# Moving the start of every large operand in on-chip memory: 32 bytes into a 256-byte line, 224 for one set of weights

## The chip, the core and the metric

The kernel runs on one core of a Trainium2 chip. The core has a matrix engine (TensorE, in the profile PE for the products and PEld for the loading of the operand that stays in the array), VectorE (DVE), ScalarE (ACT), GpSimd (POOL) and SyncE (SP), which here only issues transfers. The on-chip memory has 128 partitions; a tile's row is a run of bytes that begins at the same address in every partition. The metric is the device time of one execution in microseconds. The time before is 1136.45 us, the median of 3 runs (1136.25 to 1136.63).

## The reference

One layer of a decoder trunk on 256 tokens of 2048 features, all in float32:

```python
h = rms_norm(x, norm1_g)
proj = h @ w_in                      # 2048 x 6152: q, k, v of two groups of 8 heads, 8 forget logits
y_a = fox_attention(q_a, k_a, v_a, log_sigmoid(f_a + forget_b))
y_b = dilated_attention(q_b, k_b, v_b, rel_bias)
mixed = concat(rms_norm(y_a, outnorm_a_g), rms_norm(y_b, outnorm_b_g))
x = x + mixed @ w_out                # 2048 x 2048
h = rms_norm(x, norm2_g)
x = x + square(relu(h @ w_mlp_in)) @ w_mlp_out   # 2048 x 8192, 8192 x 2048
out = rms_norm(x, final_norm_g)
```

## The kernel before

**Products.** Every float32 matrix is split into a high and a low part of the type float32r, and each product is made of three: high by high, low by high, high by low. Activations are kept turned, with features on the partitions: `aT_hi` and `aT_lo` hold 16 blocks of 128 features by 256 tokens, `big_hi` and `big_lo` the same for the attention's output and later for the hidden layer. Weights come in steps of 256 rows by 512 columns: a transfer brings two steps into a `raw` tile, ACT copies one step into `whi` (L168), DVE subtracts to get `wlo` (L169). Both are tiles of four rotating buffers, and a step holds two blocks of 128 rows (index `j`).

In the input projection, the output projection and the down projection (L299 to L301) the weights are the *moving* operand, which streams through the array 512 columns at a time, and 128 tokens of an activation block are the *stationary* one, loaded before each product. In the up projection (L313) it is the other way: 128 columns of the weights are stationary, and the 256 tokens of a block of `aT` move. So the input projection moves `whi`/`wlo` past `aT`, output and down move `whi`/`wlo` past `big`, and up moves `aT` past `whi`/`wlo`.

**Order.** The order on every engine is written out by hand: a loop over 376 steps issues a step's products, and a table of side jobs by product (attention, norms, draining of accumulators) puts the rest between them. The splitting runs 3 steps ahead of the products, the transfers two to four steps ahead of that. The stages follow one another as input projection (with the attention of a group of heads beside the next chunks), output projection, then four rounds of up and down. The last chunk of the last down is done in three pieces; the high and low weights of its first four steps lie in the memory of `aT`, which is free by then, and its last two pieces are 256 columns wide.

**Addresses.** Tiles come from pools, and a pool's tiles lie one behind the other in the order in which they are first asked for, each rounded up to 32 bytes. So the small tiles between the large ones (norm statistics of 8 bytes, a bias of 32) decide where a large one begins. What begins where within 256 bytes, by the built program:

| operand | before | after |
|---|---|---|
| `aT_hi`, `aT_lo` | 224 | 32 |
| `big_hi`, `big_lo` | 160 | 32 |
| `whi`, `wlo` in input, output and down projection | 160 | 32 |
| `whi`, `wlo` in the up projection | 160 | 224 |
| queries, values (stationary in the attention's L493, L538) | 224 | 0 |
| keys, probabilities (moving there) | 32 | 0 |
| `xs`, identity | 128 | 0 |
| `raw` buffers | 160, 32, 160, 32 | 0, 128, 0, 128 |

All blocks within a tile lie 512, 1024 or 2048 bytes apart, so a product's operand begins at the same place of a 256-byte line as its tile. For moving / stationary this makes 160/224 in the input projection, 160/160 in output and down, 224/160 in up and 32/224 in the attention's products.

The lines that the prediction speaks of, beside L168 and L169, are these:

```python
# L299-L301, input, output, down: stationary xh/xl, moving hi/lo
nc.tensor.matmul(acc, xh, hi[:, j, cols], start=go, stop=False)
nc.tensor.matmul(acc, xl, hi[:, j, cols], start=False, stop=False)
nc.tensor.matmul(acc, xh, lo[:, j, cols], start=False, stop=end)
# L313, up: stationary 128 columns of the weights, moving 256 tokens
nc.tensor.matmul(acc, w[:, j, b * P:(b + 1) * P], a[:, kt, :], ...)
```

L538 multiplies values by probabilities (256 columns, then 128), L333 the 16 forget columns, L544 and L546 square and sum the attention's output through the tile `sqt`.

Of the kernel before, what the change touches and what calls it, by code (L numbers as in the profile page):

```python
# [11 lines left out]
F32 = mybir.dt.float32  # L12
F32R = mybir.dt.float32r
# [6 lines left out]
P = 128  # L20
# [16 lines left out]
QSCALE = HD ** -0.5  # L37

LEAD = 3
WARM, WARM2 = 8, 1  # L40


def _constants():
    i = np.arange(P)
    upto = (i[:, None] <= i[None, :]).astype(np.float32)
    after = (i[:, None] > i[None, :]).astype(np.float32)
    tri = np.where(i[None, :] <= i[:, None], 0.0, NEG).astype(np.float32)
    head = (i[:, None] % 32 == np.arange(NH)[None, :]).astype(np.float32)
    pack = np.concatenate([after, -upto, tri, np.zeros((P, P), np.float32), tri, head], axis=1)

    dist = np.arange(RW) - 127
    d = np.maximum(dist, 0)
    exact = N_BUCKETS // 2
    df = np.maximum(d.astype(np.float32), np.float32(1.0))
    large = exact + (
        np.log(df / np.float32(exact)) / np.float32(math.log(REL_MAX / exact)) * np.float32(N_BUCKETS - exact)
    ).astype(np.int32)
    bucket = np.where(d < exact, d, np.minimum(large, N_BUCKETS - 1))
    count = np.zeros(RW, np.int64)
    for window, dil in PATTERNS:  # L60
        count += (dist >= 0) & (dist % dil == 0) & (dist <= window)
# [7 lines left out]
def kernel(  # L69
# [20 lines left out]
    o2d = out.rearrange("b (t p) d -> p (b t) d", p=P)  # L90
    w_in, w_out, w_up, w_down = w_in[0], w_out[0], w_mlp_in[0], w_mlp_out[0]

    one = ctx.enter_context(tc.tile_pool(name="one", bufs=1))
    two = ctx.enter_context(tc.tile_pool(name="two", bufs=2))
    wraw = ctx.enter_context(tc.tile_pool(name="wraw", bufs=4))
    wsplit = ctx.enter_context(tc.tile_pool(name="wsplit", bufs=LEAD + 1))
    psum = ctx.enter_context(tc.tile_pool(name="psum", bufs=2, space=PSUM))
    dram = ctx.enter_context(tc.tile_pool(name="dram", bufs=1, space=DRAM))
    ctx.enter_context(tc.manual_schedule())
# [44 lines left out]
    def split(i, j0=0, n=2):  # L144
        if i >= len(steps):
            return
        if j0:
            return split_rows(i, j0, n)
        ci, s = steps[i]
        t = raws[ci, s // 2][:, 2 * (s % 2):2 * (s % 2) + 2, :]  # L150
        if ci == len(chunks) - 1 and s < 4:
            hi, lo = (a[:, 4 * s:4 * s + 4, :].rearrange("p (k j) s -> p k (j s)", k=2) for a in (aT_hi, aT_lo))
        else:
            hi, lo = (wsplit.tile([P, 2, CW], F32R, name=n) for n in ("whi", "wlo"))
        if chunks[ci][5] > CW:
# [18 lines left out]
    ident = one.tile([P, P], F32, name="ident")  # L174
    zeros = two.tile([P, CW], F32, name="nat")
    warm = zeros[:, :CW // 2].bitcast(BF16)
    half_t = one.tile([P, TB], F32, name="half_t")
    ones = one.tile([P, 1], F32, name="ones")
    nc.vector.memset(zeros[:, :CW // 2], 0.0)
    nc.vector.memset(half_t, -0.5)  # L180
    nc.vector.memset(ones, 1.0)
# [12 lines left out]
    for c in range(1, 4):  # L194
        load_x(4 * c, 4 * c + 4)
        load(2 * c)
    fb = one.tile([P, NH], F32, name="fb")
    relx = one.tile([N_BUCKETS + 1, NH], F32, name="relx")
    nc.vector.memset(relx, 1.0)
    pk = one.tile([P, 5 * P + NH], F32, name="pk")  # L200
    pick_sb = two.tile([P, RW], F32, name="pr")[:N_BUCKETS + 1]

    def small_loads():
# [4 lines left out]
        nc.sync.dma_start(pk, pack)  # L208
        nc.sync.dma_start(pick_sb, pick)

    mcat = pk[:, 2 * P:5 * P]
    head = pk[:, 5 * P:]
    gcat = one.tile([P, TB, P], F32R, name="gcat")


# [4 lines left out]
            nc.tensor.matmul(pw, warm[:, :P], warm, start=True, stop=True)  # L220

    nc.scalar.activation(ones, ones, AF.Copy)
    gT = one.tile([P, 48], F32, name="gT")

    def gains(k0, k1):
        p = psum.tile([P, 512], F32, name="tr")
        nc.tensor.transpose(p[:, :k1], grow[:k1], ident[:k1, :k1])
        nc.vector.tensor_copy(gT[:, k0:k1], p[:, k0:k1])

    aT_hi = one.tile([P, KT, SEQ], F32R, name="aT_hi")  # L230
    aT_lo = one.tile([P, KT, SEQ], F32R, name="aT_lo")

    def split_psum(hi, lo, src, scale=None):

# [20 lines left out]
    def rsqrt(dst, ssq, n):  # L255

        w = dst.shape[1]
        v = two.tile([P, TB], F32, name="rs_v")[:, :w]
        t = two.tile([P, TB], F32, name="rs_t")[:, :w]
        nc.vector.tensor_scalar(v, ssq, 1.0 / n, EPS, op0=ALU.mult, op1=ALU.add)  # L260
        nc.gpsimd.tensor_tensor(dst, v, half_t[:, :w], op=ALU.pow)
        nc.vector.tensor_tensor(t, dst, dst, op=ALU.mult)
        nc.vector.tensor_tensor(t, t, v, op=ALU.mult)
        nc.vector.tensor_scalar(t, t, -0.5, 1.5, op0=ALU.mult, op1=ALU.add)
        nc.vector.tensor_tensor(dst, dst, t, op=ALU.mult)

    ssq1 = one.tile([P, TB, 4], F32, name="ssq1")
    ssq1s = one.tile([P, TB], F32, name="ssq1s")
    rstd1 = one.tile([P, TB], F32, name="rstd1")
    rstdq = one.tile([P, TB], F32, name="rstdq")  # L270

    def first_squares(t, c):
        unused = yT_hi[:, 2 * (4 * t + c):2 * (4 * t + c) + 2, :].rearrange("p k s -> p (k s)")
# [66 lines left out]
        side.setdefault(i, []).append((f, a))  # L340


    logf = one.tile([P, TB, NH], F32, name="logf")
    lf_hi, lf_lo = (
        two.tile([P, 3 * P], F32R, name=n)[:, :2 * P].rearrange("p (t q h) -> p t q h", t=TB, q=4)
        for n in ("p_hi", "p_lo")
# [10 lines left out]
    def forget_gates():  # L357
        f = psum.tile([P, 512], F32, name="tr")
        for t in range(TB):
            nc.tensor.transpose(f[:, 2 * t * NH:2 * (t + 1) * NH], fTs[0][:, t * P:(t + 1) * P], ident[:2 * NH, :2 * NH])  # L360
        z = one.tile([P, TB, NH], F32, name="fz")
        e = one.tile([P, TB, NH], F32, name="fe")
        u = one.tile([P, TB, NH], F32, name="fu")
        d = one.tile([P, TB, NH], F32, name="fd")
        n = one.tile([P, TB, NH], F32, name="fn")
        for t in range(TB):
            for k, add in enumerate((fb, z[:, t, :])):
                nc.vector.scalar_tensor_tensor(
                    z[:, t, :], f[:, (2 * t + k) * NH:(2 * t + k + 1) * NH], rstd1[:, t:t + 1], add,
                    op0=ALU.mult, op1=ALU.add,  # L370
                )
        nc.scalar.activation(e, z, AF.Abs)
        nc.scalar.activation(e, e, AF.Exp, scale=-1.0)

        nc.vector.tensor_scalar(u, e, 1.0, None, op0=ALU.add)
        nc.vector.tensor_scalar(d, u, 1.0, None, op0=ALU.subtract)
        nc.vector.tensor_scalar(n, d, 0.0, None, op0=ALU.is_equal)
# [52 lines left out]


    qkv = {}
    yT_hi = one.tile([P, 2 * NH, SEQ], F32R, name="big_hi")
    yT_lo = one.tile([P, 2 * NH, SEQ], F32R, name="big_lo")

    def drain_v(g, ci):
        acc = accs.pop(ci)
# [41 lines left out]
    def scores(g, h):  # L479
# [17 lines left out]
        decay.pop(hd, None)  # L497
        neg = two.tile([P, 3 * P], F32, name="neg")
        pr = two.tile([P, 3 * P], F32, name="pr")
        st = two.tile([P, 3, TB], F32, name="st")  # L500
        for t, c0, c1 in spans:
            add = mcat[:, c0:c1] if kind == 0 else relT[:, hd, SEQ - (c1 - c0):]
            nc.vector.tensor_tensor_reduce(  # L503
                neg[:, c0:c1], s[:, c0:c1], add, -1.0, BIG, ALU.add, ALU.min, st[:, 0, t:t + 1]
            )
# [23 lines left out]
    def values(g, h):  # L529
# [10 lines left out]
                    start=t == 0 and n == 0, stop=t == 1 and n == 2,  # L540
                )
        first = seen[kind] == 0
        s = sq[kind] if first else two.tile([P, SEQ], F32, name="sqt")
        nc.scalar.activation(s, y[:, :SEQ], AF.Square)  # L544
        if not first:
            nc.gpsimd.tensor_tensor(sq[kind], sq[kind], s, op=ALU.add)  # L546
        split_psum(yT_hi[:, hd, :], yT_lo[:, hd, :], y[:, :SEQ], gT[:, 32 + hd:33 + hd])
        seen[kind] += 1

    rstdo = [one.tile([P, TB], F32, name=f"rstdo{k}") for k in range(2)]  # L550

    def group_norm(kind):
        p = psum.tile([P, 512], F32, name="tr")
# [2 lines left out]
                             skip_group_check=True)  # L556
        rsqrt(rstdo[kind], p[:, :TB], D_GRP)

    ssq2 = one.tile([P, TB, 4], F32, name="ssq2")
    ssq2s = one.tile([P, TB], F32, name="ssq2s")  # L560
    rstd2 = one.tile([P, TB], F32, name="rstd2")
    rstd2sq = one.tile([P, TB], F32, name="rstd2sq")

    def drain_o(kind, c, ci):
        acc = accs.pop(ci)
# [26 lines left out]
            )  # L592

    gf = relT.rearrange("p h s -> p (h s)")
    ssq3 = one.tile([P, TB, 5], F32, name="ssq3")
    ssq3s = one.tile([P, TB], F32, name="ssq3s")
    rstd3 = one.tile([P, TB], F32, name="rstd3")

    def load_gf():
        nc.sync.dma_start(  # L600
# [28 lines left out]

    def finish(t, n, cs):  # L630
        r, s = rstd3[:, t:t + 1], ssq3s[:, t:t + 1]
        v = two.tile([P, 1], F32, name="fi_v")
        u = two.tile([P, 1], F32, name="fi_u")
        ru = two.tile([P, 1], F32, name="fi_ru")
        nc.vector.tensor_scalar(v, ssq3[:, t, n:n + 1], s, 1.0 / D_MODEL, op0=ALU.add, op1=ALU.mult)
        nc.gpsimd.tensor_tensor(r, v, half_t[:, :1], op=ALU.pow)
        put_gain(t, cs)
# [145 lines left out]
```

## Time and profile before

| | |
|---|---|
| median of 3 runs | 1136.45 us (1136.25 to 1136.63) |
| the profiled execution | 1136.86 us |
| its span, first to last instruction | 1135.1 us |
| granted TensorE clock, mean | 0.998 |
| busy: PE, PEld, DVE, ACT, POOL | 99%, 87%, 56%, 46%, 3% |
| transfers | 209.15 MB, mean 184 GB/s, the hardware queue's packets 55.8% of the 16 engines |

The 1.76 us between the profiled execution and its span lie outside of the instructions. A matmul's busy time in the profile overlaps that of the next, since products are pipelined: how long one takes in a stream is read from the distance between the starts of products that follow one another, not from the mean busy time. The chain of waits and the timeline both show these starts to 0.01 us; a stretch of many gives the distance to a tenth of a nanosecond.

### The profile page before, as it was taken

Reading aid. Unit: us, or ns where it says so; the run is one execution under the profiler, and the core shown is the slowest. Engines: PE = TensorE matmul, PEld = TensorE weight load, DVE = VectorE, ACT = ScalarE, POOL = GpSimd, SP = SyncE. Lnnn points to the kernel's source line nnn. Section 1 sums busy time; section 2 is a strip of 40 time slices with the busy share of each in tenths; the row PEclk is TensorE's granted clock in tenths of the full one; section 3 lists DMA queues with packets and bytes.
Section 4 is the critical chain, followed back from the end, with each engine's and each line's share of the span. In section 5 each row is a group of like instructions: output and inputs, shape, how many; then the busy total and the mean of one; then the engine's idle time right before and its main releaser. Section 6 shows DMA issues by size and latency. Waiting matters only on the chain.

```text
span 1135.1 us, 16038 instructions
## 1 busy us (share of the span) xinstructions
PE 1124.0 (99%) x6635; PEld 988.8 (87%) x6635; DVE 639.7 (56%) x795; ACT 521.9 (46%) x675; POOL 31.7 (3%) x57
## 2 busy tenths in 40 slices
PE   9999999999999999999999999999999999999996
PEld 6778888888888889998889998889998889999886
DVE  5665656556566665555555555545555554555564
ACT  5545545545445554454334444343544433454451
POOL 0100200100001000000000000000000000000000
PEclk9999999999999999999999999999999999999999
DMA  8655454454545556556555655566465566556642
GB/s 312 224 183 183 154 185 149 149 185 149 186 156 178 155 179 192 187 179 212 196 185 164 208 186 188 200 199 192 152 220 187 186 193 192 187 171 206 240 148 74
DMA packets 104933, 209.15 MB, mean 184 GB/s; under 512 B 3651, under 2 KB 4508, under 8 KB 104732
## 3 DMA queue, kind: packets, MB, share of 16 engines
q1 hardware_dynamic: 104556, 207.06, 55.8%
q0 software_dynamic: 304, 1.06, 0.3%
q8 instruction: 52, 0.85, 0.3%
q14 instruction: 21, 0.17, 0.0%
HBM read 206.00 MB, written 2.11 MB: 183 GB/s over the span
## 4 chain that ended last, share of the span: by engine, by line
PE 98%; DMA 1%; DVE 0%; SPq 0%; ACT 0%; POOL 0%; issue 0%; DVEq 0%
PE acc L313 32%; PE acc L299 21%; PE acc L301 21%; PE acc L300 21%; PE sc L493 1%; PE sc L538 1%; PE tr L463 1%; DMA raw<-in_w_in_dram 1%; PE tr L250 1%; PE tr L520 0%; PE sc L333 0%; PE sc L490 0%; DVE wlo L169 0%; ACT whi L168 0%; DVE xs L646 0%; SPq L185 0%
## 5 line engine op out<-in xcount | busy, mean ns | idle before, releaser
L169 DVE TENSOR_TENSOR wlo<-raw,whi 128x1024 fp32r<-128x1024 f32 (+1 forms) x381 | 464.1, 1224 | 374.4 <-ACT whi L168 371.6
L168 ACT ACTIVATE whi<-raw 128x1024 fp32r<-128x1024 f32 (+1 forms) x381 | 399.8, 1055 | 404.2 <-PE acc L300 241.4
L313 PE MATMUL acc<-aT_hi,whi 128*128 128x256 f32 x1024 | 287.2, 280 | 0.0
L313 PE MATMUL acc<-aT_hi,wlo 128*128 128x256 f32 x1024 | 286.1, 279 | 0.0
L313 PE MATMUL acc<-aT_lo,whi 128*128 128x256 f32 x1024 | 286.0, 279 | 0.0
L299 PE MATMUL acc<-whi,big_hi 128*128 128x512 f32 (+1 forms) x632 | 246.0, 389 | 0.0
L301 PE MATMUL acc<-wlo,big_hi 128*128 128x512 f32 (+1 forms) x632 | 244.7, 387 | 0.0
L300 PE MATMUL acc<-whi,big_lo 128*128 128x512 f32 (+1 forms) x632 | 244.5, 387 | 0.0
L313 PEld LDWEIGHTS acc<-aT_hi,wlo 128*128 128x128 f32 x1024 | 192.8, 188 | 0.0
L313 PEld LDWEIGHTS acc<-aT_hi,whi 128*128 128x128 f32 x1024 | 192.3, 188 | 0.2
L313 PEld LDWEIGHTS acc<-aT_lo,whi 128*128 128x128 f32 x1024 | 191.6, 187 | 0.2
L299 PE MATMUL acc<-whi,aT_hi 128*128 128x512 f32 x384 | 157.0, 409 | 0.0
L300 PE MATMUL acc<-whi,aT_lo 128*128 128x512 f32 x384 | 152.5, 397 | 0.0
L301 PE MATMUL acc<-wlo,aT_hi 128*128 128x512 f32 x384 | 152.3, 397 | 0.0
L301 PEld LDWEIGHTS acc<-wlo,big_hi 128*128 128x128 f32 x632 | 118.7, 188 | 24.4
L300 PEld LDWEIGHTS acc<-whi,big_lo 128*128 128x128 f32 x632 | 118.8, 188 | 23.4
L299 PEld LDWEIGHTS acc<-whi,big_hi 128*128 128x128 f32 x632 | 118.8, 188 | 22.9
L301 PEld LDWEIGHTS acc<-wlo,aT_hi 128*128 128x128 f32 x384 | 72.5, 189 | 17.4
L299 PEld LDWEIGHTS acc<-whi,aT_hi 128*128 128x128 f32 x384 | 72.7, 189 | 15.3 <-issue 0.6
L300 PEld LDWEIGHTS acc<-whi,aT_lo 128*128 128x128 f32 x384 | 72.7, 189 | 14.0 <-DVE aT_lo L240 0.2
L237 DVE TENSOR_TENSOR big_lo<-nat,big_hi 128x512 fp32r<-128x512 f32 x32 | 22.2, 693 | 22.3 <-ACT big_hi L236 22.3
L507 ACT ACTIVATE pr<-neg,st 128x128 f32<-128x128 f32 (+1 forms) x32 | 14.3, 448 | 40.8 <-DVE st L503 40.8
(160 smaller groups left out, 533.7 us busy)
## 6 DMA issues: line engine op xcount, KB each, us to landing
raw<-in_w_mlp_in_dram SPq DMA_DIRECT2D x64, 1024.0 KB, 5.3
raw<-in_w_mlp_out_dram SPq DMA_DIRECT2D x64, 1024.0 KB, 5.2
raw<-in_w_in_dram SPq DMA_DIRECT2D x42, 1024.0 KB, 5.2
raw<-in_w_out_dram SPq DMA_DIRECT2D x16, 1024.0 KB, 5.1
raw<-in_w_in_dram SPq DMA_DIRECT2D x4, 1040.0 KB, 5.3
raw<-in_w_in_dram SPq DMA_DIRECT2D x3, 512.0 KB, 8.6
xs<-in_x_dram SPq DMA_DIRECT2D x3, 512.0 KB, 9.6
big_lo<-rel_d POOLq DMA_DIRECT2D x1, 1024.0 KB, 7.3
```

The lines of the kernel that those rows point to most:

```text
L168: nc.scalar.activation(hi, t, AF.Copy)
L169: nc.vector.tensor_tensor(lo, t, hi.bitcast(F32), op=ALU.subtract)
L237: nc.vector.tensor_tensor(lo, src, hi.bitcast(F32), op=ALU.subtract)
L250: nc.tensor.transpose(p[:, j * SEQ + t * P:j * SEQ + (t + 1) * P], xs[:, t, c:c + P], ident)
L299: nc.tensor.matmul(acc, xh, hi[:, j, cols], start=go, stop=False)
L300: nc.tensor.matmul(acc, xl, hi[:, j, cols], start=False, stop=False)
L301: nc.tensor.matmul(acc, xh, lo[:, j, cols], start=False, stop=end)
L313: nc.tensor.matmul(acc, w[:, j, b * P:(b + 1) * P], a[:, kt, :], start=kt == 0 and b % 2 == 0 and n == 0, stop=kt == kts - 1 and n == 2, s ...
L463: nc.tensor.transpose(p[:, j * SEQ + t * P:j * SEQ + (t + 1) * P], ts[t][:, h * P:(h + 1) * P], ident)
L493: nc.tensor.matmul(s[:, c0:c1], q[:, h, t * P:(t + 1) * P], k[:, h, :c1 - c0], start=n == 0 and kind == 1, stop=n == 2,)
L507: nc.scalar.activation(pr[:, c0:c1], neg[:, c0:c1], AF.Exp, bias=st[:, 0, t:t + 1], scale=-1.0, accum_out=st[:, 1, t:t + 1],)
L538: nc.tensor.matmul(y[:, o0:SEQ], v[:, t, h * P:(h + 1) * P], p[:, c0:c1], start=t == 0 and n == 0, stop=t == 1 and n == 2,)
```

## The change

Four new or changed kinds of line, and nothing else:

- Two pools are opened behind the weight buffers: `wide`, which takes `aT_hi`, `aT_lo`, `big_hi` and `big_lo`, and `few` behind it, which takes the tiles of up to 64 bytes and the constants `pk`. `wide` begins with an unused tile of 32 bytes.
- `gT` moves into a pool of its own ahead of the rest and is rounded up to 384 bytes, so that all behind it begins at a multiple of 256.
- A buffer of `whi` or `wlo` becomes 256 bytes longer, and the step's weights begin 8 elements (32 bytes) into it, or 56 elements (224 bytes) in the up projection.
- To make room, `pk` holds the causal mask once and not twice (648 columns become 520), with the mask taken as its last 128 or 256 columns, and `sqt` has one buffer and not two.

The instructions, their shapes and their order are the same on every engine. Of the waits one kind is new: ACT's Square into `sqt` (L544 before) now also waits for GpSimd's sum that read the previous one.

```diff
+LINE, NEAR, FAR = 64, 8, 56
+TURNED = "u"
...
+    lead_in = ctx.enter_context(tc.tile_pool(name="lead_in", bufs=1))
     one = ctx.enter_context(tc.tile_pool(name="one", bufs=1))
     two = ctx.enter_context(tc.tile_pool(name="two", bufs=2))
     wraw = ctx.enter_context(tc.tile_pool(name="wraw", bufs=4))
     wsplit = ctx.enter_context(tc.tile_pool(name="wsplit", bufs=LEAD + 1))
+    wide = ctx.enter_context(tc.tile_pool(name="wide", bufs=1))
+    few = ctx.enter_context(tc.tile_pool(name="few", bufs=1))
...
-            hi, lo = (wsplit.tile([P, 2, CW], F32R, name=n) for n in ("whi", "wlo"))
+            b = FAR if chunks[ci][0] in TURNED else NEAR
+            hi, lo = (
+                wsplit.tile([P, 2 * CW + LINE], F32R, name=n)[:, b:b + 2 * CW].rearrange("p (j c) -> p j c", j=2)
+                for n in ("whi", "wlo")
+            )
...
-    gT = one.tile([P, 48], F32, name="gT")
+    gT = lead_in.tile([P, 96], F32, name="gT")[:, :48]
...
-    aT_hi = one.tile([P, KT, SEQ], F32R, name="aT_hi")
-    aT_lo = one.tile([P, KT, SEQ], F32R, name="aT_lo")
+    wide.tile([P, NEAR], F32, name="ahead")
+    aT_hi = wide.tile([P, KT, SEQ], F32R, name="aT_hi")
+    aT_lo = wide.tile([P, KT, SEQ], F32R, name="aT_lo")
...
-    yT_hi = one.tile([P, 2 * NH, SEQ], F32R, name="big_hi")
-    yT_lo = one.tile([P, 2 * NH, SEQ], F32R, name="big_lo")
+    yT_hi = wide.tile([P, 2 * NH, SEQ], F32R, name="big_hi")
+    yT_lo = wide.tile([P, 2 * NH, SEQ], F32R, name="big_lo")
...
-            add = mcat[:, c0:c1] if kind == 0 else relT[:, hd, SEQ - (c1 - c0):]
+            add = (mask if kind == 0 else relT[:, hd])[:, SEQ - (c1 - c0):]
...
-        s = sq[kind] if first else two.tile([P, SEQ], F32, name="sqt")
+        s = sq[kind] if first else two.tile([P, SEQ], F32, name="sqt", bufs=1)
...
-    ssq2 = one.tile([P, TB, 4], F32, name="ssq2")
+    ssq2 = few.tile([P, TB, 4], F32, name="ssq2")
...
```

## Rows read from the trace of the kernel before

**Rows 1.** The page's head and busy shares, and one window with its granted clock.
```profile
span 1135.1 us, 16038 instructions
PE 1124.0 (99%) x6635; PEld 988.8 (87%) x6635; DVE 639.7 (56%) x795; ACT 521.9 (46%) x675; POOL 31.7 (3%) x57
...
436.00:526.00 90.00, 90.00 (x685) 86.55 (x684) 49.50 (x48) 42.81 (x49) 0.00 (x0) 1.00 0.57 188
```
**Rows 2.** The chain that ended last, share by line.
```profile
PE acc L313 32%; PE acc L299 21%; PE acc L301 21%; PE acc L300 21%; PE sc L493 1%; PE sc L538 1%; PE tr L463 1%; DMA raw<-in_w_in_dram 1%; PE tr L250 1%; PE tr L520 0%; PE sc L333 0%; PE sc L490 0%; DVE wlo L169 0%; ACT whi L168 0%; DVE xs L646 0%; SPq L185 0%
```
**Rows 3.** Costliest PE groups: count, busy and mean, idle before; one line of three.
```profile
L313 PE MATMUL acc<-aT_hi,whi 128*128 128x256 f32 x1024 | 287.2, 280 | 0.0
L299 PE MATMUL acc<-whi,big_hi 128*128 128x512 f32 (+1 forms) x632 | 246.0, 389 | 0.0
L299 PE MATMUL acc<-whi,aT_hi 128*128 128x512 f32 x384 | 157.0, 409 | 0.0
```
**Rows 4.** Chain of waits, input projection: first and last of 18 pieces.
```profile
299.98 0.23 PE acc L301
...
303.94 0.24 PE acc L300
```
**Rows 5.** The same in a down projection: first and last of 19 pieces.
```profile
569.87 0.23 PE acc L301
...
573.95 0.23 PE acc L301
```
**Rows 6.** The same in an up projection, merged to one piece.
```profile
429.94 70.08 PE acc L313 x595
```
**Rows 7.** Timeline of PE, last chunk, products of 256 weight columns; nine distances.
```profile
1117.85 0.28 PE L300 MATMUL acc<-whi,big_lo 128*128 128x256 f32 x1
...
1118.93 0.28 PE L300 MATMUL acc<-whi,big_lo 128*128 128x256 f32 x1
```
**Rows 8.** Timeline of PE, values by probabilities of one head.
```profile
114.77 0.28 PE L538 MATMUL sc<-p_hi,v_hi 128*128 128x256 f32 x1
...
115.12 0.22 PE L538 MATMUL sc<-p_hi,v_hi 128*128 128x128 f32 x1
115.18 0.27 PE L538 MATMUL sc<-p_lo,v_hi 128*128 128x128 f32 x1
115.29 0.28 PE L538 MATMUL sc<-p_hi,v_lo 128*128 128x128 f32 x1
115.41 0.45 PE L299 MATMUL acc<-whi,aT_hi 128*128 128x512 f32 x1
```
**Rows 9.** Chain of waits, the same six products of another head.
```profile
129.94 0.62 PE sc L538 x6
```
**Rows 10.** Timeline of PE, last chunk, weights in the memory of aT; nine distances.
```profile
1104.83 0.39 PE L300 MATMUL acc<-aT_hi,big_lo 128*128 128x512 f32 x1
...
1106.89 0.39 PE L300 MATMUL acc<-aT_hi,big_lo 128*128 128x512 f32 x1
```
**Rows 11.** Loading of stationary operands, groups of PEld: up, then output and down.
```profile
L313 PEld LDWEIGHTS acc<-aT_hi,wlo 128*128 128x128 f32 x1024 | 192.8, 188 | 0.0
...
L299 PEld LDWEIGHTS acc<-whi,big_hi 128*128 128x128 f32 x632 | 118.8, 188 | 22.9
```
**Rows 12.** Costliest groups of DVE and ACT: the splitting of the weights.
```profile
L169 DVE TENSOR_TENSOR wlo<-raw,whi 128x1024 fp32r<-128x1024 f32 (+1 forms) x381 | 464.1, 1224 | 374.4 <-ACT whi L168 371.6
L168 ACT ACTIVATE whi<-raw 128x1024 fp32r<-128x1024 f32 (+1 forms) x381 | 399.8, 1055 | 404.2 <-PE acc L300 241.4
```
**Rows 13.** Timeline of POOL: the shortest idle time before a sum over heads.
```profile
364.45 0.75 POOL L546 TENSOR_TENSOR sq<-sq,sqt 128x256 f32<-128x256 f32 x1 [4.55 <-ACT sqt L544]
```
**Rows 14.** Timeline of PE, the 16 forget columns as stationary operand.
```profile
52.49 0.28 PE L333 MATMUL sc<-aT_hi,wf 128*16 128x256 f32 x1
52.60 0.29 PE L333 MATMUL sc<-aT_lo,wf 128*16 128x256 f32 x1
52.73 0.39 PE L299 MATMUL acc<-whi,aT_hi 128*128 128x512 f32 x1
```

More of the change, by code (lines that the diff above doesn't have):

```diff
@@ L48, in _constants @@
     head = (i[:, None] % 32 == np.arange(NH)[None, :]).astype(np.float32)
-    pack = np.concatenate([after, -upto, tri, np.zeros((P, P), np.float32), tri, head], axis=1)
+    pack = np.concatenate([after, -upto, np.zeros((P, P), np.float32), tri, head], axis=1)
     dist = np.arange(RW) - 127
@@ L176 @@
     warm = zeros[:, :CW // 2].bitcast(BF16)
-    half_t = one.tile([P, TB], F32, name="half_t")
-    ones = one.tile([P, 1], F32, name="ones")
+    half_t = few.tile([P, TB], F32, name="half_t")
+    ones = few.tile([P, 1], F32, name="ones")
     nc.vector.memset(zeros[:, :CW // 2], 0.0)
@@ L196 @@
         load(2 * c)
-    fb = one.tile([P, NH], F32, name="fb")
-    relx = one.tile([N_BUCKETS + 1, NH], F32, name="relx")
+    fb = few.tile([P, NH], F32, name="fb")
+    relx = few.tile([N_BUCKETS + 1, NH], F32, name="relx")
     nc.vector.memset(relx, 1.0)
-    pk = one.tile([P, 5 * P + NH], F32, name="pk")
+    pk = few.tile([P, 4 * P + NH], F32, name="pk")
     pick_sb = two.tile([P, RW], F32, name="pr")[:N_BUCKETS + 1]
@@ L209, in small_loads @@
         nc.sync.dma_start(pick_sb, pick)
-    mcat = pk[:, 2 * P:5 * P]
-    head = pk[:, 5 * P:]
+    mask = pk[:, 2 * P:4 * P]
+    head = pk[:, 4 * P:]
     gcat = one.tile([P, TB, P], F32R, name="gcat")
@@ L257, in rsqrt @@
         w = dst.shape[1]
-        v = two.tile([P, TB], F32, name="rs_v")[:, :w]
-        t = two.tile([P, TB], F32, name="rs_t")[:, :w]
+        v = few.tile([P, TB], F32, name="rs_v", bufs=2)[:, :w]
+        t = few.tile([P, TB], F32, name="rs_t", bufs=2)[:, :w]
         nc.vector.tensor_scalar(v, ssq, 1.0 / n, EPS, op0=ALU.mult, op1=ALU.add)
@@ L265, in rsqrt @@
         nc.vector.tensor_tensor(dst, dst, t, op=ALU.mult)
[L267 to L270, printed above, removed]
+    ssq1 = few.tile([P, TB, 4], F32, name="ssq1")
+    ssq1s = few.tile([P, TB], F32, name="ssq1s")
+    rstd1 = few.tile([P, TB], F32, name="rstd1")
+    rstdq = few.tile([P, TB], F32, name="rstdq")
     def first_squares(t, c):
@@ L340, in at @@
         side.setdefault(i, []).append((f, a))
-    logf = one.tile([P, TB, NH], F32, name="logf")
+    logf = few.tile([P, TB, NH], F32, name="logf")
     lf_hi, lf_lo = (
@@ L360, in forget_gates @@
             nc.tensor.transpose(f[:, 2 * t * NH:2 * (t + 1) * NH], fTs[0][:, t * P:(t + 1) * P], ident[:2 * NH, :2 * NH])
[L361 to L365, printed above, removed]
+        z = few.tile([P, TB, NH], F32, name="fz")
+        e = few.tile([P, TB, NH], F32, name="fe")
+        u = few.tile([P, TB, NH], F32, name="fu")
+        d = few.tile([P, TB, NH], F32, name="fd")
+        n = few.tile([P, TB, NH], F32, name="fn")
         for t in range(TB):
@@ L499, in scores @@
         pr = two.tile([P, 3 * P], F32, name="pr")
-        st = two.tile([P, 3, TB], F32, name="st")
+        st = few.tile([P, 3, TB], F32, name="st", bufs=2)
         for t, c0, c1 in spans:
-            add = mcat[:, c0:c1] if kind == 0 else relT[:, hd, SEQ - (c1 - c0):]
+            add = (mask if kind == 0 else relT[:, hd])[:, SEQ - (c1 - c0):]
             nc.vector.tensor_tensor_reduce(
@@ L548, in values @@
         seen[kind] += 1
-    rstdo = [one.tile([P, TB], F32, name=f"rstdo{k}") for k in range(2)]
+    rstdo = [few.tile([P, TB], F32, name=f"rstdo{k}") for k in range(2)]
     def group_norm(kind):
@@ L557, in group_norm @@
         rsqrt(rstdo[kind], p[:, :TB], D_GRP)
-    ssq2 = one.tile([P, TB, 4], F32, name="ssq2")
-    ssq2s = one.tile([P, TB], F32, name="ssq2s")
-    rstd2 = one.tile([P, TB], F32, name="rstd2")
-    rstd2sq = one.tile([P, TB], F32, name="rstd2sq")
+    ssq2 = few.tile([P, TB, 4], F32, name="ssq2")
+    ssq2s = few.tile([P, TB], F32, name="ssq2s")
+    rstd2 = few.tile([P, TB], F32, name="rstd2")
+    rstd2sq = few.tile([P, TB], F32, name="rstd2sq")
     def drain_o(kind, c, ci):
@@ L594 @@
     gf = relT.rearrange("p h s -> p (h s)")
-    ssq3 = one.tile([P, TB, 5], F32, name="ssq3")
-    ssq3s = one.tile([P, TB], F32, name="ssq3s")
-    rstd3 = one.tile([P, TB], F32, name="rstd3")
+    ssq3 = few.tile([P, TB, 5], F32, name="ssq3")
+    ssq3s = few.tile([P, TB], F32, name="ssq3s")
+    rstd3 = few.tile([P, TB], F32, name="rstd3")
     def load_gf():
@@ L631, in finish @@
         r, s = rstd3[:, t:t + 1], ssq3s[:, t:t + 1]
-        v = two.tile([P, 1], F32, name="fi_v")
-        u = two.tile([P, 1], F32, name="fi_u")
-        ru = two.tile([P, 1], F32, name="fi_ru")
+        v = few.tile([P, 1], F32, name="fi_v", bufs=2)
+        u = few.tile([P, 1], F32, name="fi_u", bufs=2)
+        ru = few.tile([P, 1], F32, name="fi_ru", bufs=2)
         nc.vector.tensor_scalar(v, ssq3[:, t, n:n + 1], s, 1.0 / D_MODEL, op0=ALU.add, op1=ALU.mult)
```

## The prediction

> **What bounds the kernel now.** I read the page's head first. PE is busy 99% of the span and the granted clock of a window of 90 us is 1.00 [rows 1], so the array runs at the upper of its two levels, 2.4 GHz. The chain of waits is next: PE holds nearly all of it, 32% in L313 and 63% in L299 to L301 [rows 2]. The costliest PE groups show no idle time before them [rows 3]. So no buffer, transfer or split is waited for in bulk, and the time is the sum of the distances between products. Only something that shortens or lengthens this distance can move the time.
>
> These distances are read from the chain, where starts stand. In the input projection 17 distances take 3.96 us, 232.9 ns each [rows 4]; in a down projection 18 take 4.08 us, 226.7 ns [rows 5]; in an up projection 595 products take 70.08 us, 117.8 ns [rows 6]. If one column enters the array in each period of 2.4 GHz, 512 columns need 213.3 ns and 256 need 106.7; no stretch of equal long products here beats that. So a product carries an extra of 19.6 ns in the input projection, 13.4 in down, 11.1 in up. Two things are to be seen in them.
>
> - Input and down projection move the same weight buffers, which begin at 160. What stays in the array differs: `aT` at 224 against `big` at 160. The extra differs by 6.2 ns. The place of the stationary operand, or its relation to the moving one, costs time.
> - In the last chunk, 256 weight columns at 160 past `big` at 160 take 120.0 ns [rows 7], an extra of 13.3, the same as with 512 columns. At equal starts the extra belongs to the product and not to its columns.
>
> The nearest rows to the new starts are the attention's. Probabilities at 32 move past values at 224, which is the pair that the up projection will have. Six products, three of 256 columns and three of 128, take 0.62 us [rows 9], and the sixteen heads lie between 0.62 and 0.64. In the timeline of one head the three short ones take 0.29 us from 115.12 to 115.41 [rows 8]. With 0.63 for the six, and 0.285 for the short ones, the long ones take 115.0 ns each, an extra of 8.3. A burst of three is a short sample: the head shown has 0.35 us for three, 116.7 ns.
>
> **The change, part by part.** No instruction is added, removed or moved. The sum is made against the profiled execution's 1136.86 us, of which 1135.1 are the span; the median of the runs is 1136.45, 0.4 below.
>
> *Up projection, moving 224 to 32, stationary 160 to 224.* 3 x 1024 products [rows 3]. The pair is that of rows 8 and 9, so 115.0 ns instead of 117.8: 2.8 x 3072 = 8.6 us less. The bounds: below, a product cannot come faster than its weights are loaded. Short products, which stream for half as long, still stand 0.11 to 0.12 us apart where each needs a new load of 128 columns [rows 8], and in the up projection the loads already have no idle time between them, while down's have 22.9 us [rows 11]. With the shorter of these, 110 ns, at best 7.8 x 3072 = 24.0 us less. Above, 120.0 as in rows 7: 6.8 us more.
>
> *Output and down, 160/160 to 32/32.* 3 x 632 products less the 48 narrow ones of the last chunk leave 1848. The relation of the two starts stays, both move by 128 bytes. No row shows 512 columns at 32. The rows that bound it: unchanged at 226.7 if only the relation counts; 213.3 + 8.3 = 221.6 if the extra is that of a moving operand at 32, since by rows 5 and 7 it does not grow with the columns. Neither is nearer, so I take the middle, 224.2: 2.5 x 1848 = 4.6 us less. The outer ends are 216.6 (213.3 and the 3.3 by which the 110 of rows 8 exceeds 106.7), 18.7 us less, and the input projection's 232.9, 11.5 us more.
>
> *Input projection, 160/224 to 32/32.* 3 x 384 products. It then has the pair of output and down, so the same 224.2: 8.7 x 1152 = 10.0 us less. Its ends are 216.6, 18.8 us less, and 232.9 again, nothing.
>
> *The last chunk.* Its first four steps move from the memory of `aT`, at 224 past `big` at 160, 228.9 ns [rows 10]; some hundred products in all would lose or gain 2 to 5 ns, at most 0.6 us. I leave it out.
>
> *Where covers could go.* The array takes a step's 12 products in 2.7 us (12 x 224), and up's 24 in 2.8. One split needs 1.06 us of ACT and 1.22 of DVE [rows 12] and lies beside that; products that are 3% faster leave it covered, and a split would have to double before the array waits. The new wait of ACT's Square for GpSimd's sum costs nothing: in each case the sum before had long ended, with at least 4.55 us of idle GpSimd before the next [rows 13]. If that cover were gone, ACT's splits would queue behind the Square, and they run three steps, 8 us, ahead. Starts of the `raw` tiles, of `xs` and of the small tiles change too; transfers and small operations are not in the chain beyond 1% [rows 2], nothing is priced.
>
> *Sum.* 8.6 + 4.6 + 10.0 = 23.2 us less, 1136.9 - 23.2 = 1113.7; I say 1114.
>
> On the floor, the Trainium skill ("TensorE: Matmul & The Clock Gate", section "Back-to-back issue gap") gives N/2.4 + 2.5 ns for an isolated product, 215.8 and 109.2. An estimate by this page, with all extras gone down to 2.5, is 10.9 x 1848 + 17.1 x 1152 + 8.6 x 3072 = 66 us less, 1071. No row of this kernel comes that near, and the short products of rows 8 speak for a limit above it in up.
>
> **Rivals.**
>
> *Only the relation counts.* What matters is the distance from the moving start to the stationary one. It is 0 in output and down before and after, and 64 bytes in up (224 - 160, and 32 - 224 + 256), so these stay. Only the input projection changes, from -64 to 0, and gets down's 226.7: 6.2 x 1152 = 7.1 us less, 1129.8. For it: rows 4 against 5. Against it: rows 8 and 9 have up's relation and are 1 to 3 ns faster, though in short bursts.
>
> *The start within a line does not count.* Then the 6.2 ns of rows 4 and 5 come from something else that differs, such as the tile itself or its distance in memory from the weights, and the two forget products speak for a fixed cost: with `aT` at 224 moving and only 16 columns loaded, two of them take 0.24 us, 120 ns each [rows 14], no less than with 128. Time: 1136.9. Against it: rows 7, 8 and 6 give 120.0, 115.0 and 117.8 for the same 256 columns at three pairs of starts. The Trainium skill ("SBUF — State Buffer", section "Specifications (TRN2)") gives lines of 16 bytes: every start before and after is a multiple of 32, so by that page none should matter. The trace does not agree as it stands, 232.9 against 226.7 ns.
>
> *Slower: the new place of a long moving row is a bad one.* A row of 2048 bytes that starts at 32 ends 32 bytes into a ninth line of 256, while at 160 it reaches 160 into it; one that starts in a line's first bytes has its last piece alone. If that costs what the worst pair seen costs, output and down take the input projection's 232.9, 6.2 x 1848 = 11.5 us more, the input projection stays, and up goes to the 120.0 of rows 7, 2.2 x 3072 = 6.8 us more: 1155.2. It decides as soon as the 512-column distance passes 229.1 with up as it is, which is where the mean of 1152 at 232.9 and 1848 at 226.7 lies. For it: rows 10 have 228.9 with the moving row at 224, 2.2 more than at 160, so a start can be worse for 512 columns while it is better for 256. Against it: the probabilities at 32 are the fastest 256-column products in the trace.
>
> *Much faster.* All extras go to the outer ends: 24.0 + 18.7 + 18.8 = 61.5 us less, 1075.4. For it: nothing says that the pairs seen are near the best. Against it: no row but the weight-bound ones is that low.
>
> **How the numbers follow.** Forecast 0.57, with its own range 1092 to 1127; relation alone 0.14; no effect 0.10; slower 0.14; much faster 0.05. The range holds the forecast, the relation and no effect, and leaves out the slower case and the much faster one, 0.19: 1092 to 1137. Within 0.2%, 2.3 us, is about what a measurement of this kernel can tell from no change. Faster by more: 0.57 + 0.14 + 0.05 = 0.76; within: 0.10; slower: 0.14.
>
> **What would show it.** In the chain of waits after: up products 115 ns apart (the forecast) or 117.8 (relation alone, no effect); down 224 against 226.7 or 232.9; input projection equal to down in every case but no effect. If input and down differ still, the tile and not the start decides. If the starts of L313 stand 110 to 112 ns apart, the loading of weights bounds up. The forecast is wrong if down gets longer than 227, or if PE shows idle time ahead of its large groups, which would mean that a split, a transfer or the Square's new wait has become late. The distance of the last chunk's narrow weight products, 120.0 before, tests 256 columns at 32/32 apart from all else.

## The result and the profile after

The changed kernel takes 1128.65 us, the median of 4 runs (1128.0 to 1130.0), against 1136.54 for the kernel before, of which a fourth run stood beside them: a ratio of 0.993, 95% interval 0.9913 to 0.9948. It is faster, as forecast, but by 7.9 us and not by 23. The time lies inside the stated range, but the size is a third of the forecast's.

The profiled execution took 1130.01 us. The page's head and its PE groups are those of [rows 1, 3] with new line numbers: L312 to L314 are the input, output and down projections, L326 is up, L263 and L533 transposes, L551 values by probabilities.

```profile
span 1128.1 us, 16026 instructions
...
PE 1115.7 (99%) x6635; PEld 984.9 (87%) x6635; DVE 639.3 (57%) x795; ACT 522.1 (46%) x675; POOL 33.5 (3%) x57
...
L326 PE MATMUL acc<-aT_hi,whi 128*128 128x256 f32 x1024 | 285.1, 278 | 0.0
...
L312 PE MATMUL acc<-whi,big_hi 128*128 128x512 f32 (+1 forms) x632 | 245.8, 389 | 0.0
...
L312 PE MATMUL acc<-whi,aT_hi 128*128 128x512 f32 x384 | 155.3, 404 | 0.1
```

PE still has no idle time before its large groups, and the busy times of DVE and ACT are within half a microsecond of what they were: no cover went. So the answer lies in the distances again. First the chain of waits in an undisturbed stretch of the input projection, the counterpart of [rows 4], first and last of 94 pieces.

```profile
291.88 0.23 PE acc L313
...
312.96 0.23 PE acc L313
```

93 distances take 21.08 us, 226.7 ns, where [rows 4] have 232.9. Then a down projection, as [rows 5], first and last of 19 pieces.

```profile
565.85 0.23 PE acc L314
...
569.93 0.23 PE acc L314
```

18 distances in 4.08 us: 226.7 ns, what it was before to a tenth. The up projection, as [rows 6], in two of its four rounds.

```profile
419.96 75.14 PE acc L326 x663
...
599.90 70.19 PE acc L326 x596
```

Here is the surprise: 113.3 ns a product in the first round and 117.8 in the second, with the same starts, the same instructions and the same tiles. Rounds three and four are like the second. The timeline shows where the first round changes.

```profile
413.92 0.28 PE L326 MATMUL acc<-aT_hi,wlo 128*128 128x256 f32 x1
414.04 0.60 PE L263 MATMUL tr<-ident,xs 128*128 128x128 f32 x4
414.39 0.36 PE L326 MATMUL acc<-aT_hi,whi 128*128 128x256 f32 x1
414.60 0.28 PE L326 MATMUL acc<-aT_lo,whi 128*128 128x256 f32 x1
414.71 0.28 PE L326 MATMUL acc<-aT_hi,wlo 128*128 128x256 f32 x1
...
415.50 0.28 PE L326 MATMUL acc<-aT_hi,whi 128*128 128x256 f32 x1
```

The products ahead of the four transposes of the norm's work stand 117.8 apart; behind them seven distances from 414.71 to 415.50 take 0.79 us, 113 ns. A second burst of four transposes, at 415.85, changes nothing, and 113.3 stays until the down projection. The next view is the chain where attention work stands between the products of the input projection.

```profile
123.04 0.64 PE sc L551 x6
123.68 0.29 PE acc L312
123.97 0.24 PE acc L313
124.21 0.23 PE acc L314
124.44 0.24 PE acc L312
124.67 0.23 PE acc L313
124.91 0.23 PE acc L314
125.13 0.23 PE acc L312
```

Behind a head's six products the four distances from 123.97 to 124.91 take 0.94 us, 235 ns each, though the starts are right; in this trace it takes about a dozen products, at 224 to 240 ns, until they stand at 226.7 again. Over the whole input projection from its second chunk on, without the two products that come first behind another kind, the mean goes from 233.3 to 228.5 ns, and 70% of them stand at 224 to 228. What that is worth is read from the first product of the second chunk and the first of the output projection, before and after:

```profile
35.11 0.39 PE L299 MATMUL acc<-whi,aT_hi 128*128 128x512 f32 x1
...
316.15 0.39 PE L299 MATMUL acc<-whi,big_hi 128*128 128x512 f32 x1
```

```profile
36.02 0.39 PE L312 MATMUL acc<-whi,aT_hi 128*128 128x512 f32 x1
...
312.57 0.39 PE L312 MATMUL acc<-whi,big_hi 128*128 128x512 f32 x1
```

That is 281.04 us before and 276.55 after, 4.5 less.

One thing is this execution's own: PE stood idle for 2.21 us in the first chunk (0.82 in the trace of the kernel before), and the granted clock of the window of 12 to 16 us is 0.57, so for most of it the array ran at the lower of its two levels, 1.2 GHz.

```profile
12.38 0.69 PE L263 MATMUL tr<-ident,xs 128*128 128x128 f32 x2 [2.21 <-DVE aT_lo L253]
...
12.00:16.00 4.00, 3.62 (x11) 2.94 (x12) 2.42 (x4) 1.42 (x2) 0.00 (x0) 0.57 1.05 409
```

Its second chunk begins at 36.02 us, in a later execution of the same kernel (`after_again`) at 34.84, and that 1.2 us is the whole difference of the two spans, 1128.1 and 1127.0.

### The profile page after: what moved, and what is told of

It reads as the page before. It is cut to its first block, busy times and chain, and to the rows that moved or that the text cites. A ratio compares the mean times of both kernels' runs of the same rounds, so it can differ in the third digit from the quotient of the medians.

```text
span 1128.1 us, 16026 instructions
## 1 busy us (share of the span) xinstructions
PE 1115.7 (99%) x6635; PEld 984.9 (87%) x6635; DVE 639.3 (57%) x795; ACT 522.1 (46%) x675; POOL 33.5 (3%) x57
## 4 chain that ended last, share of the span: by engine, by line
PE 98%; DMA 1%; DVE 0%; SPq 0%; ACT 0%; POOL 0%; issue 0%; DVEq 0%
PE acc L326 32%; PE acc L312 21%; PE acc L314 21%; PE acc L313 21%; PE sc L506 1%; PE sc L551 1%; PE tr L476 1%; PE tr L263 1%; DMA raw<-in_w_in_dram 1%; PE tr L533 0%; PE sc L346 0%; PE sc L503 0%; DVE wlo L181 0%; ACT whi L180 0%; DVE xs L659 0%; SPq L197 0%
## 5 line engine op out<-in xcount | busy, mean ns | idle before, releaser
L326 PE MATMUL acc<-aT_hi,wlo 128*128 128x256 f32 x1024 | 285.7, 279 | 0.0
L326 PE MATMUL acc<-aT_hi,whi 128*128 128x256 f32 x1024 | 285.1, 278 | 0.0
L326 PE MATMUL acc<-aT_lo,whi 128*128 128x256 f32 x1024 | 285.0, 278 | 0.0
L312 PE MATMUL acc<-whi,big_hi 128*128 128x512 f32 (+1 forms) x632 | 245.8, 389 | 0.0
L314 PE MATMUL acc<-wlo,big_hi 128*128 128x512 f32 (+1 forms) x632 | 244.4, 387 | 0.0
L326 PEld LDWEIGHTS acc<-aT_lo,whi 128*128 128x128 f32 x1024 | 192.5, 188 | 0.1
L326 PEld LDWEIGHTS acc<-aT_hi,wlo 128*128 128x128 f32 x1024 | 192.2, 188 | 0.0
L326 PEld LDWEIGHTS acc<-aT_hi,whi 128*128 128x128 f32 x1024 | 191.7, 187 | 0.2
L312 PE MATMUL acc<-whi,aT_hi 128*128 128x512 f32 x384 | 155.3, 404 | 0.1
L314 PE MATMUL acc<-wlo,aT_hi 128*128 128x512 f32 x384 | 150.6, 392 | 0.0
L314 PEld LDWEIGHTS acc<-wlo,big_hi 128*128 128x128 f32 x632 | 118.7, 188 | 24.3
L312 PEld LDWEIGHTS acc<-whi,big_hi 128*128 128x128 f32 x632 | 118.8, 188 | 23.2
L314 PEld LDWEIGHTS acc<-wlo,aT_hi 128*128 128x128 f32 x384 | 72.4, 189 | 16.0
L312 PEld LDWEIGHTS acc<-whi,aT_hi 128*128 128x128 f32 x384 | 72.6, 189 | 14.1 <-ACT fu L393 0.6
```

## The experiments

A step's start can be set chunk by chunk, so one kernel measures many pairs of starts; each chunk gives its distance over its 96 products (down) or 192 (up) by itself. "Relation" is the moving start minus the stationary one, modulo 256. Where a diff only sets starts, the function `start_of` gives the byte at which a chunk's weights begin; the activations begin at 32 where nothing else is said.

**Sweeps of the starts: `sweep_32` and `sweep_160`.**

```diff
+def start_of(what, key):
+    if what in "ud":
+        r, c = key
+        return (4 * r + c) % 8 * 32
...
-            b = FAR if chunks[ci][0] in TURNED else NEAR
+            b = ((start_of(*chunks[ci][:2]) - 0) % 256) // 4
```

> Activations begin at 32 as in the changed kernel; the weights' start runs through 0, 32, ... 224 from chunk to chunk of the up and down projections. Every chunk computes what it did. Relation theory (what counts is moving start minus stationary start, modulo 256): down chunks with weights at 32 stay at 226.7 ns (relation 0), those with weights at 224 (relation -64) take the input projection's old 232.9; up chunks with weights at 224 take 116.5 (relation +64), those with weights at 32 take 120.0 (relation 0). Moving-start theory (the start of the streaming operand alone counts): all up chunks alike at 116.5, since the 256 tokens always start at 32, and down chunks differ, 226.7 at 32 and at 160. Tile theory (no start counts, the tiles do): all down chunks 226.7 and all up chunks 116.5.

> The same sweep of the weights' starts with the activations at 160. Relation theory: the same eight distances as with the activations at 32, only turned by 128 bytes: down at 226.7 with weights at 160, up at 116.5 to 117.8 with weights at 96 and 120.0 with weights at 160. Moving-start theory: all up chunks alike at 120 (as the last chunk's 256 columns at 160), and down chunks as in the sweep with activations at 32, weight start by weight start. Tile theory: no differences.

They took 1142.97 and 1143.17 us; the output projection's starts ran through the same values. Distances in ns by relation:

| relation | 0 | 32 | 64 | 96 | 128 | 160 | 192 | 224 |
|---|---|---|---|---|---|---|---|---|
| 512 columns, activations at 32 | 226.7 | 233.3 | 228.9 | 233.3 | 233.3 | 234.3 | 233.3 | 233.3 |
| 512 columns, activations at 160 | 226.7 | 233.3 | 228.9 | 233.3 | 233.3 | 234.3 | 233.3 | 233.3 |
| 256 columns, activations at 32 | 120.0 | 116.7 | 117.8 | 120.0 | 118.7 | 118.7 | 117.8 | 118.3 |
| 256 columns, activations at 160 | 120.0 | 116.7 | 113.3, 117.8 | 120.0 | 118.7, 120.0 | 118.7 | 117.8 | 118.3 |

Moved by 128 bytes, the curve stays: the relation decides. A relation that comes once as a positive and once as a negative difference (160 = 192 - 32, and -96 = 64 - 160, both 234.3 with 512 columns) gives the same, so the curve repeats after 256 bytes; after 128 it does not (226.7 at 0, 233.3 at 128). The moving-start theory, on which my price of output and down stood, and with it that of the input projection, falls, and so does the tile theory. The rows of the kernel before lie on the curve too, within half a nanosecond: relation 192 in [rows 4], 0 in [rows 5, 7], 64 in [rows 6, 10]. Two cells have two values, in chunks with the same starts. The chain in `sweep_160`, first the one chunk at relation 64, then the other:

```profile
483.90 16.21 PE acc L336 x143
...
843.94 16.14 PE acc L336 x137
```

113.4 and 117.8.

**All up at 32, `up_near`; all moved by 128, `rel_160`; the input projection undone, `in_far`.**

```diff
# up_near
+    return 32
# rel_160, activations at 160
+    return 96 if what == "u" else 160
# in_far
+    if what in "qkv":
+        return 224
+    return 224 if what == "u" else 32
```

> The changed kernel with the up projection's weights at 32 as all others, so up has 32/32. Relation theory: 120.0 ns for 3072 products instead of 116.5, 10.8 us more than the changed kernel's 1128.7: about 1139. Moving-start theory: the tokens still start at 32, no change: 1128.7.

> The changed kernel with everything moved by 128 bytes: 160/160 in the input, output and down projections, 160/96 in up. Relation theory: as the changed kernel, 1128.7, or up to 4 us more if up's 117.8 against 116.5 comes from the place in the line. Moving-start theory: input stays at 232.9 as before (moving at 160 in both), output and down as before, up 120 (moving at 160): about 1143.

> The changed kernel with one part undone: the input projection's weights begin at 224, so moving minus stationary is 192 there, as before the change, and all else stays. Relation theory: the input projection goes back from 226.7 to 233 ns in its undisturbed stretches, 5 to 7.7 us more than the changed kernel: 1133.7 to 1136.4. Moving-start theory (224 is a worse start than 160 for 512 columns, 2 ns): as before the change or more. Tile theory: no change from 1128.7.

| | us | ratio to before, 95% |
|---|---|---|
| `up_near` | 1138.84 | 1.0007 to 1.0026 |
| `rel_160` | 1132.06 | 0.9943 to 0.9973 |
| `in_far` | 1133.38 | 0.9958 to 0.9979 |

The kernel before has 1137.0 beside them. `up_near` came as the relation theory had it, and its up projection shows 120.0:

```profile
599.90 70.20 PE acc L330 x585
```

`rel_160` has the input projection's gain alone, 5.0 us: all its up rounds run at 117.8, the first too, which has the same transposes as the changed kernel's; why they do not turn it there is not shown. `in_far` keeps 3.65 us against the kernel before, just under the 1133.7 that the relation theory gave it at the least: its first up round still runs at 113.3, and its input projection is back. In their traces the input projection from its second chunk on takes 276.6 us in `rel_160`, as in the changed kernel, and 281.2 in `in_far`, where the kernel before has 281.0. So it is worth 4.5 us, and not the 7.1 of 6.2 ns times 1152, because of the disturbed stretches. Most of the rest of the differences between runs lies in the first chunk, which is 27.2 to 29.6 us long in these traces.

**Finer relations, `sweep_fine` and `fine2`.** Both set the relation of each chunk from a list.

```diff
+    if what == "u":
+        r, c = key
+        rel = (4, 8, 16, 24, 40, 48, 56, 60, 68, 72, 80, 88, 112, 208, 240, 248)[4 * r + c]
+        return (32 - rel) % 256
```

> Activations at 32; the weights' starts run through relations (moving minus stationary) between the multiples of 32: in the 16 up chunks 4, 8, 16, 24, 40, 48, 56, 60, 68, 72, 80, 88, 112, 208, 240, 248 bytes, in the down chunks 4, 8, 16, 24, -4, -8, -16, -24, 48, 56, 72, 80, 12, -12, 0. If the memory's unit is 32 bytes, relations inside one unit (4 to 24) act as 0 or 32: 120.0 or 116.7 in up, 226.7 or 233.3 in down. If it is smaller, values in between appear. Moving-start theory: up chunks all alike.

> Sixteen further relations in the up chunks (252, 244, 236, 228, 12, 20, 28, 36, 44, 52, 76, 100, 120, 140, 180, 200) and fifteen in the down chunks (60, 68, 76, 100, 116, 120, 136, 144, 152, 176, 200, 208, 28, 36, 44). So far 248 in up has 115.6, without a second rhythm seen, and no relation in down is under the 226.7 of 0 and -4. If the relation works by single elements, neighbours of 248 differ by some nanoseconds from it; a relation with less than 115.6 in up or less than 226.7 in down would beat the changed kernel by (117.8 - x) x 2304 less 2.2 x 768 or by (226.7 - x) x 1848.

They took 1141.8 and 1142.87 us. With 512 columns, relation 0 gives 226.7, 4 gives 236.7, 8 gives 233.3, 12 gives 228.9, 28 and 60 and 252 give 226.7, 100 and 244 give 240.0. There is no unit of 32 bytes; one element more moves it by up to 10 ns (from 0 to 4), the whole curve spans 13, and nothing measured is under 226.7. With 256 columns most lie between 115.6 (248) and 120.7 (36), and two are at 113.3 after their first ten products: 76 and 180. Each of these chunks was entered once, so a second distance of a relation could have gone unseen. The chain in the chunk at 76:

```profile
824.89 15.19 PE acc L338 x134
```

**Fewer columns loaded, `narrow`.**

```diff
-        xh, xl = (p[:, base + kt, t * P:(t + 1) * P] for p in (ah, al))
+        xh, xl = (p[:, base + kt, t * P:t * P + m] for p in (ah, al))
+        acc = acc[:m]
...
+        m = (128, 96, 64, 32)[key[1]] if what == "d" else P
```

> Leaves out work: in the down chunks c = 0, 1, 2, 3 of a round only the first 128, 96, 64, 32 tokens of a block are loaded as stationary operand, all 512 columns still move; rounds 0 and 3 at relation 0, round 1 at -64 (192), round 2 at 128. Collision theory (the moving stream loses time while the load of the next stationary operand reads the same memory): the extra falls with the columns loaded, at relation 0 from 13.3 to about 10, 6.7 and 3.3 ns (226.7, 223, 220, 217), at -64 from 20 to 15, 10, 5 (233, 228, 223, 218). Fixed-cost theory (the starts set a cost per product, whatever is loaded): 226.7 and 233.3 in every chunk of the round.

| columns loaded | 128 | 96 | 64 | 32 |
|---|---|---|---|---|
| relation 0, round 1 | 226.7 | 230.0 | 230.0 | 231.7 |
| relation 192, round 2 | 233.3 | 228.3 | 232.6 | 231.7 |
| relation 128, round 3 | 232.2 | 231.6 | 229.3 | 230.6 |

Neither theory holds. Round 4, at relation 0 again, repeats round 1 as far as it goes (226.7, 230.0, 230.0). With fewer columns loaded the distance changes, but the extra does not shrink with them: a quarter of the load makes relation 0 worse by 5 ns. The picture of two readers that take each other's turns, so many per column, falls. The edit narrows the written result to the same number of rows (`acc[:m]`), so which of the two moves the distance is not shown. (1187.18 us in all; the accumulators were cleared first, and PE waited for it.)

**What chooses between 113.3 and 117.8: `kick`, `kick2`, `kick_sweep`, `probe`.** All add products that nobody uses to the up chunks of the changed kernel.

```diff
# kick: at the head of each later chunk, n = 16 to 512 columns
+                nc.tensor.matmul(p[:, :n], aT_hi[:, 0, :P], ..., start=True, stop=True)
# kick2: after 24 products of rounds 2, 3, 4; kick_sweep: in every chunk, with many relations
+                nc.tensor.transpose(p[:, m * P:(m + 1) * P], xs[:, 0, m * P:(m + 1) * P], ident)
# probe: twelve kinds and places, after product n of column block 3
+            (1, 0): ("t", 4, (1,), 2), (1, 1): ("t", 4, (1, 2), 2), (1, 2): ("t", 3, (1,), 2), ...
```

> The changed kernel, in whose profile the first round of up chunks ran at 113.3 ns and the other three at 117.8 with the same starts. Here one unused product of 16, 32, 48, 64, 96, 128, 160, 192, 224, 256, 384 or 512 columns stands at the head of each of the 12 later up chunks. Lock theory (the two streams settle into one of two rhythms, and how a stretch is entered chooses it): some of the 12 chunks run at 113.3 and some at 117.8, with nothing between. Beside-work theory (the first round is faster since other work runs or lacks beside it): the first round at 113.3, all 12 others at 117.8 whatever the unused product.

> The changed kernel with unused fp32 transposes after the first 24 products of the up projection's rounds 2, 3 and 4 (4, 1 and 2 of them, 0.11 us each); in round 1 four transposes of the norm's work stand there already, and the trace shows 118 ns before them and 113.3 behind. Lock theory (the transposes change how far ahead of a product its stationary operand is loaded, and the stream keeps that rhythm): rounds 2 to 4 go from 117.8 to 113.3 behind their transposes, at least with four; 4.44 x 744 = 3.3 us a round less, 8 to 10 us in all if every round follows: about 1120. Beside-work theory: rounds 2 to 4 stay at 117.8 and the time rises by some 0.9 us to about 1130.

> Sixteen relations of the starts in the up chunks (0, 32, 64, 96, 128, 160, 192, 224, 4, 8, 16, 48, 56, 72, 240, 248) and fifteen in the down chunks (0, -4, 12, 32, 64, 88, 96, 128, 160, 192, 224, 80, 16, 48, -8), each chunk with four unused transposes after its first 24 (up) or 12 (down) products. Lock theory: a relation can have more than one steady distance; some chunks differ from those of the sweeps without transposes (120.0, 116.7, 117.8, 120.0, 118.7, 118.7, 117.8, 118.3 in up; 226.7, 233.3, 228.8 in down), relation 64 in up gives 113.3. Relation theory in its simple form (one distance for a relation): the same values as without the transposes.

> The changed kernel with unused products in the middle of the second block of each of the 12 later up chunks, at different places: transposes as in the norm's work (3, 4 or 8 of them, once or twice), one to four of them between the three products of a group, and one to four products of 128 columns of aT. Lock theory: what chooses the rhythm is the exact distance at which the disturbance falls into the stream's pattern of three products, so some of the 12 places turn 117.8 into 113.3 and others do not, and a chunk keeps what the one before had if it is not turned. Beside-work theory: none does, all 12 chunks stay at 117.8.

`kick`: 1130.07 us. First round 113.3, none of the twelve later chunks turned. That was the beside-work theory's result. `kick2`: 1129.72 us, and again the rounds stay at 117.8 behind four transposes at the very place where the first round has them:

```profile
587.99 0.12 PE acc L330
588.11 0.44 PE tr L343 x4
588.55 15.55 PE acc L330 x132
```

15.55 us for 132 are 117.8. Twice my lock theory had missed. `kick_sweep` (1152.56 us) spoke for it. Its chunk at relation 64 goes from 117.7 to 113.4 at the four transposes:

```profile
456.98 3.06 PE acc L338 x26
460.04 0.44 PE tr L351 x4
460.48 17.57 PE acc L338 x155
```

Relation 192, 117.8 in both sweeps, ran at 113.3, but it did so after its first five products, ahead of its transposes: there the entry from the chunk before decided, and not they. Relation 16 went the other way, from 117.3 to 120.0. `probe` (1134.35 us) decides. In the second chunk of round 2 (four transposes after each of two blocks) the distance falls behind the first four, in the third (three transposes) it rises again; the chain behind each:

```profile
615.18 14.85 PE acc L348 x131
...
635.91 18.14 PE acc L348 x154
```

113.4 and 117.8, with no other work beside these than beside the ten chunks that kept 117.8. So both rhythms are open to the same starts, in round 2 as in round 1, a disturbance can turn one into the other both ways, and most do not: the first chunk of round 2 has the same four transposes at the same product and keeps 117.8. What exactly a disturbance must hit stays open.

**Relations that find the short rhythm: `up_76`, `up_180`, beside `after_again`.**

```diff
# up_76
+    return (32 - 76) % 256 if what == "u" else 32
# up_180
+    return (32 - 180) % 256 if what == "u" else 32
```

> The changed kernel with the up projection's weights at 212, relation 76. In the sweep one chunk at 76 went by itself from 115.9 to 113.3 within its first quarter. If 76 always ends in 113.3 whatever precedes it: 4.44 x 2304 = 10.2 us less than the changed kernel, 1118.4. If its rhythm too depends on what precedes it, some rounds run at 118 or so: 1122 to 1129.

> The same with the weights at 108, relation 180, of which one chunk in the sweep went from 114.4 to 113.3. As for 76: 1118.4 if 113.3 is reached from any entry, 1122 to 1129 if not.

> The changed kernel itself, on the chip of the two runs beside it: 1128.0 to 1130.0. If the first round alone runs at 113.3 again, the choice of the rhythm is fixed by the program; if other rounds do, it is chance from run to run.

| | us | ratio to before, 95% |
|---|---|---|
| `up_76` | 1121.94 | 0.9854 to 0.9886 |
| `up_180` | 1118.57 | 0.9826 to 0.9854 |
| `after_again` | 1128.84 | 0.9918 to 0.9946 |

The kernel before has 1137.04 here. `after_again` has its first round at 113.3 and the others at 117.8 once more: that split belongs to the program and is not chance. With relation 76 the rhythm depends on what comes before too, only the other way round: its first round goes to 118.2 behind the second burst of transposes and stays there, the others run at 113.3.

```profile
413.01 1.39 PE acc L330 x12
414.40 0.44 PE tr L267 x4
414.83 19.27 PE acc L330 x163
...
434.94 65.12 PE acc L330 x551
...
589.93 80.13 PE acc L330 x707
```

Relation 180 was at 113.3 in every chunk of all four rounds. Each round settles there within its first six products, and the first again behind both bursts of transposes:

```profile
432.99 62.11 PE acc L330 x548
...
590.00 15.07 PE acc L330 x133
```

With 4.44 ns less on 2304 products, 10.2 us, the changed kernel's 1128.84 becomes 1118.6: measured 1118.57. It beats both kernels, by 18.5 and 10.3 us. That it settles from every possible entry is not shown, only from those of this program and from the one in `fine2`.

## Why the prediction was wrong in size

*What bounds the kernel, and that the extra belongs to the pair of starts:* right. Outside the first chunk, what is gained is in the distances between products; nothing became late, the new wait included. The step that failed is the price of the starts: it took the moving operand's start for the cause in three projections, and a burst's distance for the only one of its pair in the up projection.

*Output and down, 4.6 us less:* wrong, 0. This step carried the extra of 8.3 ns from 256 columns to 512 by the equality of [rows 5] and [rows 7]. That equality holds at relation 0 alone (13.3 both); at relation 32 the extras are 20.0 and 10.0, so an extra read with 256 columns says nothing about 512. And it held the moving start for the cause, where the sweeps show the relation, which the change leaves at 0 here. The test that the prediction had named, the last chunk's narrow products at 32/32, says the same: nine distances in 1.08 us, 120.0 ns as in [rows 7].

```profile
1117.29 0.28 PE L312 MATMUL acc<-whi,big_hi 128*128 128x256 f32 x1
...
1118.37 0.28 PE L312 MATMUL acc<-whi,big_hi 128*128 128x256 f32 x1
```

*Input projection, 10.0 us less:* 4.5. The rival's 226.7 is what undisturbed stretches have, not 224.2. The step counted all 1152 products at one distance; 30% of those measured stand behind attention work or transposes, at 229 to 240.

*Up, 8.6 us less:* 3.3, which is 4.44 ns on the 744 products of one round that stand behind its first transposes. The 115.0 of [rows 8, 9] was taken for a steady distance of the pair 32/224. It is none: the pair has the two rhythms 113.3 and 117.8, and in a burst of three products there is no steady one. I had named the short sample and still set the term on it.

The sum by these is 0 + 4.5 + 3.3 = 7.8, measured 7.9, and 8.2 in `after_again`. The rival "only the relation counts", given 0.14, named the relation and had 1129.8. That it came so near in time is in part luck: it had the input projection 2.6 us too large and lacked the 3.3 of the first up round, which no rival had. Against it I had held the bursts, and they were the weak rows. The rival that no start counts is refuted, also what it took from the Trainium skill's lines of 16 bytes ("SBUF — State Buffer", section "Specifications (TRN2)"): starts that are multiples of 32 bytes do differ, 226.7 at relation 0 and 233.3 at 32. The slower rival priced a place in a line, and no place counts by itself, as far as 32 against 160 tests it; its price for up, 120.0, is that of relation 0, and `up_near` shows what it would have cost.

## What to carry to other kernels

When products stand back to back, read their distance from starts, and compare it for each pair of tiles: here two streams that differ only in where their rows begin differ by 3 to 6%, and the start of the weights can be set chunk by chunk, so that one run measures a whole curve. A distance from a burst of three, or from another number of columns, is no price for a long stream. Take a relation into use only after seeing that every round of the real program runs at its short rhythm.

## What was not expected of the hardware

- A stream of products has rhythms: the distance in an undisturbed chunk is constant to 0.01 ns from chunk to chunk (226.66 to 226.67, 117.77 to 117.79), a pair of starts can have two such distances (113.33 and 117.78 at relations 64 and 192), and in the changed kernel's first round the one that was entered lasts through the three further chunks.
- The relation works by single elements (226.7 at 0, 236.7 at 4 bytes, 226.7 at 28), differently for 256 and 512 columns, and the extra does not shrink when fewer columns are loaded (`narrow`). Which circuit makes it so is not shown by these runs.
